# Two stacked transformer blocks on one core: weights in units of two K tiles, x loaded first, and a first layer in five phases

## The chip, the cores and the metric

One core of a Trainium2 chip runs the whole program. The metric is the device time of one execution in microseconds (us). TensorE (PE in the rows) multiplies, VectorE (DVE) and ScalarE (ACT) work on elements, GpSimd (POOL) does little here, and SyncE (SP) issues nearly all loads, in one queue and in order.

## The reference

The input `x` is 256 tokens by 2048 features in float32. Two layers of a first block and two layers of a second block follow each other. The change is in the first block, whose layers begin like this:

```python
mod = jax.nn.silu(c) @ w_mod + b_mod                  # 2048 -> 3 * 2048, one row for all tokens
shift, scale, gate = jnp.split(mod, 3, axis=-1)
h = rms_norm(x, g_pre) * (1.0 + scale[:, None, :]) + shift[:, None, :]
proj = h @ w_in                                       # 2048 -> 5648 columns
...                                                   # attention, gating and linear attention on parts of proj
out = y @ w_out
return x + gate[:, None, :] * rms_norm(out, g_post)
```

The second block has attention of three kinds and an MLP (`w_up`, `w_down`); its share of the time is the larger one, and its code is only re-indented by the change.

## The kernel before, in words

The 2048 features are 16 K tiles of 128. A product needs a K tile of `h` (feature-major, `hT`) and the same K tile of the weight. Weights come as float32 by loads of two K tiles by 512 columns (512 KB) into `raw`, a ring of five buffers. ScalarE rounds a load to `hi` (L265), VectorE takes `lo = raw - hi` (L266), and TensorE adds three products (L287 to L289: hi, lo, and hi with the low half of `hT`). A few K tiles of layer 0, `WHOLE0 = (3, 7, 11, 14, 15)`, are multiplied whole in float32 instead (L325), without a split.

`shift`, `scale` and `gate` are products of one row with `w_mod`, by a generator `gemv`. Each of its loads goes into `rawm`, a ring of two buffers, or, ahead of the first phase, into `raw`. VectorE multiplies each K tile of the load by a scalar of `sc` and adds it to `gacc` (L493, the first of a row by L491). When all 16 K tiles of the input are in, TensorE sums `gacc` over partitions (L498), and VectorE adds the bias (L507, `mod`). A variant, `gemv_pe`, lets TensorE do the whole product (L523).

Layer 0 of the first block runs its input product in phases of K tiles: `[(0,), (4,), (8,), (12,)]`, where 4 stands for K tiles 4 to 7. In each phase but the last, eleven column chunks of `w_in` (nine of 512 columns, two of 264) are multiplied. The first phase copies its sums out of PSUM on ScalarE (L819), each later one adds them on VectorE (L821, 24 instructions a phase: 18 of 512 columns and 6 narrower ones). Three chunks before the end of a phase, `enter(p + 1)` drains the background work, starts the `gemv` loads for the K tiles of the phase after, transposes `x` (L747), scales it (L751, `h`) and makes `hT` (L755, L759, L760), which needs `scale` for L751 and `shift` for the rest. `pump`, called after each unit of weights, gives out background loads at a set rate. The last phase has all chunks and the mixing between them.

Ahead of the first phase, `scale` for K tiles 0 to 3 is made by `gemv` on VectorE, `shift` for K tiles 0 and 1 by `gemv_pe`, `x` is loaded behind twelve of these loads, and `shift` for K tiles 2 and 3 follows by `gemv`. A list scheduler sets the order of instructions on each engine when the program is built, so the order isn't that of the code.

Of the kernel before, what the change touches and what calls it, by code (L numbers as in the profile page):

```python
# [21 lines left out]
P = 128  # L22
# [68 lines left out]
def kernel(  # L91
# [44 lines left out]
    # ---------------------------------------------------------------- constants  # L136
# [19 lines left out]
    # vectors that scale features, feature-major  # L156
# [3 lines left out]
    def fm_load(g, parts, on=None):  # L160
        """parts: (names, [rows, 128] AP); the rows become columns of fm, from 128 g on."""
# [31 lines left out]
    # vectors along the free axis  # L193
# [36 lines left out]
    # ---------------------------------------------------------------- helpers  # L230
# [13 lines left out]
    def put(dst, ps, scale=None):  # L244
        """dst (hi | lo) from a [128, 256] view of PSUM."""
# [23 lines left out]
    def w_unit(w, k0, n0, n, whole=()):  # L269
        """4 K tiles x n columns of w, split but for those in whole; yields (kt, [(hi [128, n], lo), ...])."""  # L270
        for k in range(k0, k0 + 4, 2):
            raw = raw_tile()
            nc.sync.dma_start(
                out=raw[:, :2 * n].rearrange("p (k n) -> p k n", k=2),
                in_=w[k * P:(k + 2) * P, n0:n0 + n].rearrange("(k p) n -> p k n", p=P))
            js = [j for j in range(2) if k + j not in whole]
            parts = [(raw[:, j * n:(j + 1) * n], None) for j in range(2)]
            if js:
                o = js[0] * n
                hi, lo = split(raw[:, o:o + len(js) * n], len(js) * n)  # L280
                for i, j in enumerate(js):
                    parts[j] = hi[:, i * n:(i + 1) * n], lo[:, i * n:(i + 1) * n]
            yield (k, parts)

    def three(ps, xa, xb, wh, wl, first, last):
        """(xa + xb)^T (wh + wl) onto ps."""
        PE.matmul(ps, lhsT=xa, rhs=wh, start=first, stop=False)  # L287
        PE.matmul(ps, lhsT=xa, rhs=wl, start=False, stop=False)  # L288
        PE.matmul(ps, lhsT=xb, rhs=wh, start=False, stop=last)  # L289

    late = []
    AGE = 3

    def settle(age=0):
        """the last step of each gemv whose loads were all given out at least age pumps ago."""
        while late and bg["n"] - late[0][0] >= age:
            late.pop(0)[1]()
# [19 lines left out]
    def gemm_chunk(w, xT, units, n0, n, after_unit=None, whole=()):  # L317
        ps = [bank(mm) for _ in range(2)]
        for k0 in units:
            for kk, pairs in w_unit(w, k0, n0, n, whole):  # L320
                for t in range(2):
                    for j, (wh, wl) in enumerate(pairs):
                        a = xT[kk + j]
                        if wl is None:
                            PE.matmul(ps[t][:, :n], lhsT=a[:, t * P:(t + 1) * P], rhs=wh, start=kk + j == units[0],  # L325
                                      stop=kk + j == units[-1] + 3)
                            continue
                        three(ps[t][:, :n], a[:, 0, t * P:(t + 1) * P], a[:, 1, t * P:(t + 1) * P],
                              wh, wl, kk + j == units[0], kk + j == units[-1] + 3)
# [31 lines left out]
    def turn(srcs, eng, m=None, tag="k"):  # L361
        """transposes of up to 4 [128, 128] APs, side by side."""
# [10 lines left out]
    def y_turn(dst, ytm):  # L373
        """ytm: per token tile a [128, 512]; dst: 4 act tiles."""
# [10 lines left out]
    def x_done(t, n):  # L385
        """the sum of squares of a finished 512-column piece of x."""
# [10 lines left out]
    # rotary tables of the first block  # L397
# [61 lines left out]
    def rotate(buf, nh, cos2, sin2, hf):  # L459
        """in place on buf [128, nh, 2 * hf]; sin2 = (-sin | sin)."""  # L460
# [52 lines left out]
    def gemv_pe(l, part, k0, nk, tag, pb):  # L513
        """the same on the tensor engine, a K tile of the result after the other, into a bank."""
        for i in range(nk):
            n0 = part * D + (k0 + i) * P
            for u in range(0, KT, 8):
                raw = raw_tile(tag)
                nc.sync.dma_start(
                    out=raw.rearrange("p (k n) -> p k n", k=8),  # L520
                    in_=w_mod[l, u * P:(u + 8) * P, n0:n0 + P].rearrange("(k p) n -> p k n", p=P))
                for k in range(8):
                    PE.matmul(pb[:, i:i + 1], lhsT=raw[:, k * P:(k + 1) * P], rhs=sc[:, u + k:u + k + 1],  # L523
                              start=(u + k == 0), stop=(u + k == KT - 1))
                yield

    # ---------------------------------------------------------------- first block
# [9 lines left out]
    def swa(l, cc, q, kv, kT, zs, yT):  # L537
        """heads 8 cc .. 8 cc + 7."""
# [832 lines left out]
```

## Time and profile before

| what | us |
|---|---|
| three timed runs | 3045.58, 3048.32 (median), 3050.96 |
| span of the profiled execution | 3045.1 |
| TensorE busy in that span | 2953.5 (97%) |
| VectorE busy | 1984.3 (65%) |
| ScalarE busy | 1436.1 (47%) |

The profiled execution is known by its span, from the first to the last instruction; its own time lies between that and the runs beside it, the median of which is 3.2 above the span. Shares of busy time are means over all stages. A busy TensorE isn't one at its peak, since the ends of its pipelined products are modelled.

### The profile page before, as it was taken

The page shows a single profiled execution, that of the slowest core. Times are in us where ns is not written, and L with a number is a line of the kernel's source. Part 1 is how long each engine was busy: PE and PEld are TensorE (multiplying, and loading weights), DVE is VectorE, ACT ScalarE, POOL GpSimd, SP SyncE. Part 2 cuts the span into 40 slices and gives each one's busy share as a digit, 9 for nine tenths or more (in the row PEclk, how much of TensorE's full clock was granted, in tenths as well). Part 3 has the DMA queues.
Part 4 walks back from the last instruction along what each step waited for, and adds up shares of the span by engine and source line. Part 5 has one row for each costly group of instructions (what it writes and reads, how often), then busy time and mean ns, then how long its engine had stood idle before and what let it go on. Part 6 is the DMA issues. An engine that isn't in the chain of part 4 may idle for free.

```text
span 3045.1 us, 40015 instructions
## 1 busy us (share of the span) xinstructions
PE 2953.5 (97%) x15042; PEld 2442.3 (80%) x15042; DVE 1984.3 (65%) x2832; ACT 1436.1 (47%) x2271; POOL 36.3 (1%) x56
## 2 busy tenths in 40 slices
PE   6999998999999999999999999999999999999998
PEld 5676676887787887888888888888788888888887
DVE  5888877788766555565666656656555665656655
ACT  2334545445556555454444444455554444444444
POOL 0000000000000000000000000000000000000000
PEclk9999998999999999999999999999999999999999
DMA  8898588898454655565665566554556666555564
GB/s 286 291 317 291 184 266 288 279 309 269 123 180 146 180 145 163 175 188 192 189 191 188 190 190 190 190 173 135 166 165 199 192 188 190 190 190 190 188 191 153
DMA packets 318072, 617.57 MB, mean 203 GB/s; under 512 B 20233, under 2 KB 48069, under 8 KB 317877
## 3 DMA queue, kind: packets, MB, share of 16 engines
q1 hardware_dynamic: 317220, 614.40, 63.4%
q8 instruction: 118, 1.93, 0.3%
q0 software_dynamic: 336, 0.49, 0.1%
q14 instruction: 78, 0.63, 0.1%
q10 hardware_dynamic: 320, 0.12, 0.0%
HBM read 610.73 MB, written 4.19 MB: 202 GB/s over the span
## 4 chain that ended last, share of the span: by engine, by line
PE 80%; DMA 8%; DVE 7%; issue 2%; ACT 2%; POOL 0%; SPq 0%; DVEq 0%; ACTq 0%; POOLq 0%
PE b L288 16%; PE b L289 16%; PE b L287 16%; PE b L1190 16%; PE b L1192 8%; DMA rawm<-in_w_mod_dram 5%; DVE gacc L493 2%; DVE lo L266 2%; PE b L325 1%; DMA raw<-in_w_in_dram 1%; PE b L366 1%; ACT hi L265 1%; PE b L564 1%; PE b L952 1%; PE b L551 0%
## 5 line engine op out<-in xcount | busy, mean ns | idle before, releaser
L266 DVE TENSOR_TENSOR lo<-raw,hi 128x1024 fp32r<-128x1024 f32 (+4 forms) x964 | 1126.6, 1170 | 799.0 <-ACT hi L265 795.7
L265 ACT CAST hi<-raw 128x1024 fp32r<-128x1024 f32 (+4 forms) x964 | 972.7, 1009 | 1313.5 <-PE b L289 758.1
L287 PE MATMUL b<-hi,act 128*128 128x512 f32 (+2 forms) x2728 | 1072.9, 394 | 9.2 <-DVE pr L821 2.6
L288 PE MATMUL b<-lo,act 128*128 128x512 f32 (+2 forms) x2728 | 1047.7, 384 | 6.9 <-DVE lo L266 6.8
L289 PE MATMUL b<-hi,act 128*128 128x512 f32 (+2 forms) x2728 | 1045.5, 384 | 0.3 <-DVE act L252 0.3
L1190 PE MATMUL b<-act,hi 128*128 128x512 f32 x2048 | 721.0, 397 | 0.0
L287 PEld LDWEIGHTS b<-hi,act 128*128 128x128 f32 x2728 | 515.1, 189 | 121.2 <-issue 16.4
L288 PEld LDWEIGHTS b<-lo,act 128*128 128x128 f32 x2728 | 515.7, 189 | 117.1 <-DVE lo L266 11.7
L289 PEld LDWEIGHTS b<-hi,act 128*128 128x128 f32 x2728 | 514.9, 189 | 98.1 <-issue 1.2
L1192 PE MATMUL b<-act,lo 128*128 128x256 f32 x2048 | 574.9, 281 | 0.0
L1190 PEld LDWEIGHTS b<-act,hi 128*128 128x128 f32 x2048 | 384.4, 188 | 92.8
L1192 PEld LDWEIGHTS b<-act,lo 128*128 128x128 f32 x2048 | 386.9, 189 | 0.5
L493 DVE SCALAR_TENSOR_TENSOR gacc<-rawm,sc,gacc 128x1024 f32<-128x1024 f32 (+1 forms) x210 | 220.9, 1052 | 57.7 <-DMA rawm<-in_w_mod_dram 56.2
L325 PE MATMUL b<-raw,act 128*128 128x512 f32 (+1 forms) x240 | 111.0, 561 | 0.0
L1208 DVE SCALAR_TENSOR_TENSOR act<-b,s,act 128x512 f32<-128x512 f32 x128 | 90.0, 744 | 5.7 <-PE b L289 5.7
L354 ACT ACTIVATE s<-s,s 128x128 f32<-128x128 f32 (+3 forms) x144 | 64.1, 447 | 40.3 <-DVE s L351 39.3
L241 POOL TENSOR_TENSOR s<-s,cs 128x1 f32<-128x1 f32 (+1 forms) x38 | 27.6, 730 | 2909.0 <-DVE s L239 2709.3
L325 PEld LDWEIGHTS b<-raw,act 128*128 128x128 f32 x240 | 43.8, 191 | 17.9 <-issue 11.8
L1200 DVE SCALAR_TENSOR_TENSOR h<-h 128x256 f32<-128x256 f32 x128 | 54.4, 425 | 4.4
L821 DVE TENSOR_TENSOR act<-b,act 128x512 f32<-128x512 f32 (+2 forms) x82 | 51.4, 632 | 8.2 <-PE b L325 7.4
L390 ACT ACTIVATE junk<-act 128x512 bf16<-128x512 f32 x56 | 35.1, 626 | 40.2 <-DMA act<-in_x_dram 21.1
L1198 DVE TENSOR_TENSOR h<-b,h 128x256 f32<-128x256 f32 x128 | 53.4, 417 | 0.0
(268 smaller groups left out, 1666.7 us busy)
## 6 DMA issues: line engine op xcount, KB each, us to landing
raw<-in_w_in_dram SPq DMA_DIRECT2D x256, 512.0 KB, 4.8
raw<-in_w_up_dram SPq DMA_DIRECT2D x256, 512.0 KB, 3.7
raw<-in_w_down_dram SPq DMA_DIRECT2D x256, 512.0 KB, 3.6
rawm<-in_w_mod_dram SPq DMA_DIRECT2D x176, 512.0 KB, 4.8
raw<-in_w_out_dram SPq DMA_DIRECT2D x64, 512.0 KB, 4.7
raw<-in_w_o_dram SPq DMA_DIRECT2D x64, 512.0 KB, 3.7
raw<-in_w_in_dram SPq DMA_DIRECT2D x32, 288.0 KB, 2.9
raw<-in_w_in_dram SPq DMA_DIRECT2D x32, 264.0 KB, 4.7
```

Source lines behind the costliest of these rows:

```text
L265: A.copy(out=hi[:, :n], in_=src)
L266: V.tensor_tensor(out=lo[:, :n], in0=src, in1=hi[:, :n].bitcast(F32), op=SUB)
L287: PE.matmul(ps, lhsT=xa, rhs=wh, start=first, stop=False)
L288: PE.matmul(ps, lhsT=xa, rhs=wl, start=False, stop=False)
L289: PE.matmul(ps, lhsT=xb, rhs=wh, start=False, stop=last)
L325: PE.matmul(ps[t][:, :n], lhsT=a[:, t * P:(t + 1) * P], rhs=wh, start=kk + j == units[0], stop=kk + j == units[-1] + 3)
L354: A.activation(out=s[:, h, :], in_=s[:, h, :], func=AF.Exp, bias=nm[:, h:h + 1], accum_out=den[:, h:h + 1])
L493: eng.scalar_tensor_tensor(out=acc, in0=w, scalar=sc[:, u + k:u + k + 1], in1=acc, op0=MUL, op1=ADD)
L1190: PE.matmul(ps[f], lhsT=wh[:, f * P:(f + 1) * P], rhs=a.rearrange("p a b -> p (a b)"), start=(kk + j == 0), stop=False)
L1192: PE.matmul(ps[f][:, S:], lhsT=wl[:, f * P:(f + 1) * P], rhs=a[:, 0, :], start=False, stop=(kk + j == KT - 1))
L1200: V.scalar_tensor_tensor(out=s2, in0=s, scalar=0.0, in1=s, op0=MAX, op1=MUL)
L1208: V.scalar_tensor_tensor(out=xc, in0=ps, scalar=r2[t], in1=xc, op0=MUL, op1=ADD)
```

## The change

Five things change.

- `w_unit`, four K tiles in two loads, becomes `w_pair`, two K tiles in one load. Loads, splits and products are the same; `pump` is now called after every two K tiles, and the rates (`UN1`, `RATE0`, `RATE1`) and `AGE` are set so that a K tile gives out as much as before.
- Layer 0 runs in five phases: K tiles 0 and 1; 2 and 3; 4 to 7; 8 to 11; 12 to 15.
- `x` is loaded ahead of all `w_mod`.
- Ahead of the first phase, `scale` and `shift` are made for K tiles 0 and 1 alone, `scale` by `gemv` on VectorE, `shift` by a new `gemv_pe` with two columns groups a load. Together they take 8 loads in place of 16.
- `scale` and `shift` of K tiles 2 and 3 become the background of the first phase (8 loads, each of four K tiles by 256 columns), those of K tiles 4 to 7 the background of the second (16 loads), and so on.

```diff
@@ the rate of background work, and its age
-    AGE = 3
+    AGE = 6
@@ gemm_chunk
-        for k0 in units:
-            for kk, pairs in w_unit(w, k0, n0, n, whole):
-                for t in range(2):
...
+        for kk in units:
+            pairs = w_pair(w, kk, n0, n, whole)
+            for t in range(2):
...
@@ shift on the tensor engine
-    def gemv_pe(l, part, k0, nk, tag, pb):
-        for i in range(nk):
-            n0 = part * D + (k0 + i) * P
-            for u in range(0, KT, 8):
...
+    def gemv_pe(l, part, k0, tag, pbs):
+        nk = len(pbs)
+        n, n0 = nk * P, part * D + k0 * P
+        per = 1024 // n
...
+        for u in range(0, KT, per):
+            raw = raw_tile(tag)
...
+            for k in range(per):
+                for i in range(nk):
+                    PE.matmul(pbs[i][:, 0:1], lhsT=raw[:, k * n + i * P:k * n + (i + 1) * P],
+                              rhs=sc[:, u + k:u + k + 1], start=(u + k == 0), stop=(u + k == KT - 1))
+            yield
@@ prepare0
-        if p == 0:
-            background(mods(0, 1, (4, 4)) + mods(0, 0, (4, 4)), 16 / UN0)
...
+        if p < 4:
+            if p == 1:
+                fill_rope()
+                fill_vectors()
+            k0, nk = ((2, 2), (4, 4), (8, 4), (12, 4))[p]
+            pumps = 8 * len(PHASES0[p])
+            background(mods(0, 1, (k0, nk)) + mods(0, 0, (k0, nk)), 4 * nk / (1.125 * pumps))
@@ the start
-    UN0 = 9
-    UN1 = 24
-    RATE1 = 48
-    NPE = 2
-    RATE0 = 31
+    PHASES0 = [(0,), (2,), (4, 6), (8, 10), (12, 14)]
+    UN1 = 48
+    RATE1 = 96
+    RATE0 = 62
...
-    pb = bank()
-    scale, shift = mods(0, 1, (0, 4), tag="raw")[0], gemv_pe(0, 0, 0, NPE, "raw", pb)
+    x_load(x[0])
+    pbs = [bank() for _ in range(2)]
+    scale, shift = mods(0, 1, (0, 2), tag="raw")[0], gemv_pe(0, 0, 0, "raw", pbs)
     for i in range(4):
         next(scale)
         next(shift, None)
+    for n in range(4):
+        for t in range(2):
+            x_done(t, n)
     fill_fm(None)
     run([scale])
-    x_load(x[0])
-    for n in range(4):
-        for t in range(2):
-            x_done(t, n)
-    run([gemv(0, 0, NPE, 4 - NPE, V, "raw", pb[:, NPE:])])
-    mod_done(0, 0, 0, 4, pb)
+    for i in range(2):
+        mod_done(0, 0, i, 1, pbs[i])
...
-        block1(0, [(0,), (4,), (8,), (12,)], SPLIT0, ORDER, prepare0, lambda: None, WHOLE0)
+        block1(0, PHASES0, SPLIT0, ORDER, prepare0, lambda: None, WHOLE0)
```

What the scheduler makes of it is seen in the order of instructions. First the load queue (SyncE) at the start of the program, before; `raw` tiles of L485 are `scale` by `gemv`, those of L519 `shift` by `gemv_pe`, `act` tiles are pieces of `x`:

```order
L168 DMA y_88<-in_c_dram 16x128
L485 DMA raw_104<-in_w_mod_dram 128x2x512
L519 DMA raw_108<-in_w_mod_dram 128x8x128
...
L485 DMA raw_187<-in_w_mod_dram 128x2x512
L154 DMA act_198<-in_x_dram 128x512
...
L485 DMA raw_244<-in_w_mod_dram 128x4x256
L273 DMA raw_307<-in_w_in_dram 128x2x512
```

The same place now (L484 is `gemv`, L521 `gemv_pe`, L272 `w_in`):

```order
L168 DMA y_88<-in_c_dram 16x128
L154 DMA act_101<-in_x_dram 128x512
...
L154 DMA act_115<-in_x_dram 128x512
L484 DMA raw_121<-in_w_mod_dram 128x4x256
L521 DMA raw_128<-in_w_mod_dram 128x4x256
...
L521 DMA raw_176<-in_w_mod_dram 128x4x256
L272 DMA raw_258<-in_w_in_dram 128x2x512
```

All eight pieces of `x` now stand ahead of eight loads of `w_mod`, where twelve stood ahead of `x` and four behind it.

Second, TensorE at the start, before: L523 is `shift`, L173 transposes vectors, L747 `x`, L768 spreads the reciprocal norms, L425 transposes the positions, L208 the rows of `sg_b`, one instruction a layer:

```order
L523 MATMUL b_101<-sc,raw_108 128x1 x8
L173 MATMUL b_163<-cs,y_160 128x128
L173 MATMUL b_172<-cs,y_166 128x104
L523 MATMUL b_101<-sc,raw_122 128x1 x8
L523 MATMUL b_101<-sc,raw_136 128x1 x8
L523 MATMUL b_101<-sc,raw_150 128x1 x8
L747 MATMUL b_276<-cs,act_198 128x128
...
L425 MATMUL b_694<-cs,y_692 128x2
L208 MATMUL b_738<-cs,y_736 128x8
L208 MATMUL b_743<-cs,y_741 128x8
```

And now (L526 is `shift`, L771 and L424 what L768 and L425 were):

```order
L526 MATMUL b_118<-sc,raw_128 128x1
L173 MATMUL b_199<-cs,y_196 128x128
L173 MATMUL b_208<-cs,y_202 128x104
L771 MATMUL b_232<-h_233,cs 128x128
L771 MATMUL b_232<-h_236,cs 128x128
L424 MATMUL b_513<-cs,y_511 128x2
L208 MATMUL b_557<-cs,y_555 128x8
L208 MATMUL b_562<-cs,y_560 128x8
L526 MATMUL b_117<-sc,raw_144 128x1
```

The spreading of the norms, the positions and both `sg_b` transposes moved from behind all four loads of `shift` to a place between the first and the second of them.

Third, VectorE where the first half of a phase of four K tiles comes ready: `mod_0` is `shift`, `act` with L760 the low half of `hT` of K tiles 4 to 6. Before, the 19th of the 22 `w_in` loads of the phase ahead is split (`lo_823`) just before it:

```order
L493 SCALAR_TENSOR_TENSOR gacc_562<-rawm_680,sc,gacc_562 128x512
L455 COPY rope<-s_725 128x8 x2
L751 SCALAR_TENSOR_TENSOR h_771<-b_761,mod_1_102,rb_274 128x256
L266 TENSOR_TENSOR lo_823<-raw_820,hi_822 128x1024
L507 TENSOR_TENSOR mod_0_224<-b_684,fm 128x4
L491 TENSOR_SCALAR gacc_809<-rawm_810,sc 128x512
L266 TENSOR_TENSOR lo_841<-raw_838,hi_840 128x512
L760 SCALAR_TENSOR_TENSOR act_753<-h_751,mod_0_224,act_753 128x256
```

Now (L492 is the accumulation, L824 the addition, L506 the bias, L763 the low half of `hT`), for the same K tiles:

```order
L266 TENSOR_TENSOR lo_951<-raw_948,hi_950 128x512
L492 SCALAR_TENSOR_TENSOR gacc_736<-rawm_789,sc,gacc_736 128x512
L824 TENSOR_TENSOR act_636<-b_923,act_636 128x512
L266 TENSOR_TENSOR lo_973<-raw_970,hi_972 128x1024
...
L824 TENSOR_TENSOR act_670<-b_947,act_670 128x512
L492 SCALAR_TENSOR_TENSOR gacc_736<-rawm_815,sc,gacc_736 128x512
L266 TENSOR_TENSOR lo_995<-raw_992,hi_994 128x512
L266 TENSOR_TENSOR lo_1017<-raw_1014,hi_1016 128x1024
L492 SCALAR_TENSOR_TENSOR gacc_736<-rawm_839,sc,gacc_736 128x512 x2
L506 TENSOR_TENSOR mod_0_127<-b_870,fm 128x4
L763 SCALAR_TENSOR_TENSOR act_883<-h_881,mod_0_127,act_883 128x256
```

`lo_951` belongs to the last `w_in` load of the second phase, `lo_973`, `lo_995` and `lo_1017` already to the third, which needs this `shift`: it now comes behind all splits and all 24 additions of the phase ahead.

From the first `h` (L751, now L754) to this `shift`, VectorE's queue held, before, 30 accumulations of 512 columns and 13 of 256 with 2 that begin a row, 19 splits and no addition. It now holds 30 of 512 and 30 of 256 with 4 that begin a row, 25 splits (11 of 1024 columns, 2 of 528, 10 of 512, 2 of 264), 24 additions, 11 instructions of 256 columns on `h` and `hT`, and some 35 small ones.

## Rows read from the trace of the kernel before

**Rows 1.** The page, busy time of each engine, share of the span, instructions.
```profile
PE 2953.5 (97%) x15042; PEld 2442.3 (80%) x15042; DVE 1984.3 (65%) x2832; ACT 1436.1 (47%) x2271; POOL 36.3 (1%) x56
```

**Rows 2.** Windows: stretch, length, busy per engine, clock, DMA share, GB/s.
```profile
0.00:50.50 50.50, 24.16 (x106) 21.94 (x106) 26.15 (x59) 11.39 (x25) 4.17 (x11) 1.00 0.91 284
50.50:117.30 66.80, 65.02 (x271) 47.29 (x270) 51.50 (x102) 30.46 (x55) 0.00 (x0) 1.00 0.88 298
117.30:184.40 67.10, 63.47 (x259) 45.63 (x258) 55.80 (x88) 19.25 (x28) 0.00 (x0) 0.97 0.86 291
184.40:245.80 61.40, 61.30 (x264) 45.21 (x263) 55.25 (x85) 17.67 (x26) 0.00 (x0) 1.00 0.92 316
```

**Rows 3.** Timeline: start, length, what; first product, last additions of two phases.
```profile
50.47 0.78 PE L287 MATMUL b<-hi,act 128*128 128x512 f32 x1
...
184.41 0.68 DVE L821 TENSOR_TENSOR act<-b,act 128x512 f32<-128x512 f32 x1
...
245.75 0.69 DVE L821 TENSOR_TENSOR act<-b,act 128x512 f32<-128x512 f32 x1 [0.87 <-PE b L325]
```

**Rows 4.** TensorE's waits, 50 to 246: total, times, longest; first and last of six.
```profile
PE b L287 <- DVE act L821: 1.8, 2, 1.6
...
PE b L747 <- DVE mod L507: 0.3, 1, 0.3
```

**Rows 5.** Waits of VectorE and of the load queue, 50 to 246; landing of `rawm`.
```profile
DVE lo L266 <- ACT hi L265: 12.2, 15, 2.0
DVE gacc L493 <- DMA rawm<-in_w_mod_dram: 10.9, 12, 2.4
DVE act L821 <- PE b L325: 5.4, 8, 1.9
...
SPq L485 <- DVE gacc L493: 86.0, 45, 4.8
...
DMA to landing us min/median/max: 3.7/4.4/7.5
```

**Rows 6.** Timeline of the start; the last row is the landing of `sg_b`.
```profile
9.90 3.54 PE L523 MATMUL b<-sc,raw 128*128 128x1 f32 x16 [5.56 <-DMA raw<-in_w_mod_dram]
13.31 0.63 PE L173 MATMUL b<-cs,y 128*128 128x128 f32 x2
14.05 0.51 POOL L206 DMA_DIRECT2D y<-in_sg_b_dram  x1 [4.79 <-PE b L173]
38.29 0.48 DVE L751 SCALAR_TENSOR_TENSOR h<-b,mod,rb 128x256 f32<-128x256 f32 x1
49.70 0.16 DVE L507 TENSOR_TENSOR mod<-b,fm 128x4 f32<-128x4 f32 x1 [1.10 <-PE b L498]
...
DMA to landing us min/median/max: 4.4/4.7/5.0
```

**Rows 7.** Groups on VectorE, 184.4 to 245.8; the last row 0 to 50.5.
```profile
L493 DVE SCALAR_TENSOR_TENSOR gacc<-rawm,sc,gacc 128x512 f32<-128x512 f32 x23 | 17.1, 745 | 1.8 <-DMA rawm<-in_w_mod_dram 1.6
L821 DVE TENSOR_TENSOR act<-b,act 128x512 f32<-128x512 f32 x17 | 11.7, 687 | 2.4 <-PE b L325 2.3
L266 DVE TENSOR_TENSOR lo<-raw,hi 128x1024 fp32r<-128x1024 f32 x9 | 11.0, 1218 | 0.2 <-ACT hi L265 0.2
...
L266 DVE TENSOR_TENSOR lo<-raw,hi 128x512 fp32r<-128x512 f32 x8 | 5.5, 685 | 0.7 <-ACT hi L265 0.5
...
L493 DVE SCALAR_TENSOR_TENSOR gacc<-raw,sc,gacc 128x256 f32<-128x256 f32 x15 | 7.2, 480 | 0.1
```

**Rows 8.** TensorE after a wait: one timeline row, then a window as in rows 2.
```profile
149.10 0.39 PE L287 MATMUL b<-hi,act 128*128 128x264 f32 x1 [1.58 <-DVE act L821]
...
147.00:153.00 6.00, 4.42 (x22) 3.91 (x20) 4.90 (x10) 1.51 (x2) 0.00 (x0) 0.72 0.79 264
```

**Rows 9.** TensorE's waits from 246 to 1000, the largest of 21.
```profile
PE b L288 <- DVE lo L266: 6.1, 6, 1.9
```

**Rows 10.** A window as in rows 2, in layer 1.
```profile
900.00:950.00 50.00, 50.00 (x244) 41.83 (x244) 25.13 (x33) 27.02 (x42) 0.00 (x0) 1.00 0.65 204
```

More of the change, by code (lines that the diff above doesn't have):

```diff
@@ L267, in split, with w_pair @@
         return hi, lo
[L269 to L283, printed above, removed]
+    def w_pair(w, k, n0, n, whole=()):
+        raw = raw_tile()
+        nc.sync.dma_start(
+            out=raw[:, :2 * n].rearrange("p (k n) -> p k n", k=2),
+            in_=w[k * P:(k + 2) * P, n0:n0 + n].rearrange("(k p) n -> p k n", p=P))
+        js = [j for j in range(2) if k + j not in whole]
+        parts = [(raw[:, j * n:(j + 1) * n], None) for j in range(2)]
+        if js:
+            o = js[0] * n
+            hi, lo = split(raw[:, o:o + len(js) * n], len(js) * n)
+            for i, j in enumerate(js):
+                parts[j] = hi[:, i * n:(i + 1) * n], lo[:, i * n:(i + 1) * n]
+        return parts
     def three(ps, xa, xb, wh, wl, first, last):
@@ L318, in gemm_chunk @@
         ps = [bank(mm) for _ in range(2)]
-        for k0 in units:
-            for kk, pairs in w_unit(w, k0, n0, n, whole):
-                for t in range(2):
[L322 to L329, printed above, removed]
+        for kk in units:
+            pairs = w_pair(w, kk, n0, n, whole)
+            for t in range(2):
+                for j, (wh, wl) in enumerate(pairs):
+                    a = xT[kk + j]
+                    if wl is None:
+                        PE.matmul(ps[t][:, :n], lhsT=a[:, t * P:(t + 1) * P], rhs=wh, start=kk + j == units[0],
+                                  stop=kk + j == units[-1] + 1)
+                        continue
+                    three(ps[t][:, :n], a[:, 0, t * P:(t + 1) * P], a[:, 1, t * P:(t + 1) * P],
+                          wh, wl, kk + j == units[0], kk + j == units[-1] + 1)
             if after_unit:
@@ L511, in mod_done @@
             V.tensor_tensor(out=o, in0=o, in1=fv(("gpost", l), k0, nk), op=MUL)
-    def gemv_pe(l, part, k0, nk, tag, pb):
-        for i in range(nk):
-            n0 = part * D + (k0 + i) * P
-            for u in range(0, KT, 8):
[L518 to L525, printed above, removed]
+    def gemv_pe(l, part, k0, tag, pbs):
+        nk = len(pbs)
+        n, n0 = nk * P, part * D + k0 * P
+        per = 1024 // n
+        if (l, part) not in mod:
+            mod[l, part] = const.tile([P, KT], F32, name=f"mod{l}_{part}")
+        for u in range(0, KT, per):
+            raw = raw_tile(tag)
+            nc.sync.dma_start(
+                out=raw.rearrange("p (k n) -> p k n", k=per),
+                in_=w_mod[l, u * P:(u + per) * P, n0:n0 + n].rearrange("(k p) n -> p k n", p=P))
+            for k in range(per):
[3 more added lines that the diff above has]
+            yield
     def swa_keys(kv):
@@ L853, in enter @@
             prepare(p)
-            for k0 in phases[p]:
-                make_hT(l, k0 // 4, rb, hT, whole)
+            for k in phases[p]:
+                make_hT(l, k, rb, hT, whole)
         enter(0)
@@ L960, in block2 @@
     def block2(l, xT, r):
-        units = (0, 4, 8, 12)
+        units = tuple(range(0, KT, 2))
         mix = {}
```

72 lines of the change are left out of this document (33 added, 39 removed).

## The prediction, made before the run

> **What bounds the kernel now.** The page comes first: TensorE is busy for 2953.5 of 3045.1 us [rows 1], so 91.6 us are open in the whole program. The windows by stage come second. Before the first product of layer 0, at 50.5, TensorE is idle for 26.3 us, more than a quarter of all that is open; in the three phases that follow it is busy for 65.0 of 66.8, 63.5 of 67.1 and 61.3 of 61.4 us [rows 2]. I set the ends of the phases at their last copies or additions, 117.3, 184.4 and 245.8 [rows 3]. The reader should see two more things in those windows: the DMA share is 0.86 to 0.92, and VectorE is busy for 51.5, 55.8 and 55.3 us, so three resources run close to each other.
>
> The waits come third. From 50 to 246 TensorE waits for 5.6 us in all, over six kinds of wait [rows 4]; it sets the pace, by a narrow margin. VectorE waits for hi casts, for `rawm` loads and for TensorE, some 31 us together. The load queue issued 53 `rawm` loads there, and 45 times it stood until VectorE was done with a buffer, 86 us in all; a load then takes 4.4 us to land [rows 5]. So both `rawm` buffers are always in use, and the modulation can't run ahead by itself: it goes as fast as VectorE empties them.
>
> A head start of TensorE is therefore worth something only if VectorE's modulation for the next phase is ready earlier too. That is what I work out.
>
> **The start.** Removed: eight `w_mod` loads, 4.2 MB, ahead of the first phase. Moved: `x`. Before, `h` begins at 38.29, but `shift` for K tiles 2 and 3 is only there at 49.70, and the first product follows [rows 3, 6].
>
> Now, step by step. The constants and `x`, 2.3 MB, at the 284 GB/s of the first stretch [rows 2] take 8.1 us from the first issue, at about 1.7: all landed at 9.8. Two `w_mod` loads more, 1.05 MB, 3.7 us: 13.5. The first load of `shift` keeps TensorE for 3.5 us, as one did before (16 records) [rows 6]: 17.0. Then TensorE's order has the two L173, and six small instructions, the second L208 among them, ahead of the other loads of `shift`. That L208 needs the second `sg_b` load, which GpSimd gave out 0.74 us after L173 began and which takes at least 4.4 us to land [rows 6]: 17.0 + 0.7 + 4.7 = 22.4. Behind this wait stand twenty-four matmuls of three `shift` loads, and behind them the load queue, as the fourth load takes the buffer that the second one frees. The second load's products end at 25.9; the fourth load is given out then and lands 4.4 to 4.7 later, at about 30.6; the third load's products and a few transposes fill the time to 30.3; the fourth's end at 34.1. Half a microsecond for L497 and about 0.9 for five short VectorE instructions brings `h` to 35.5. One `h`, one activation and one hi cast later, at about 37.5, comes the first product. The head start of TensorE is 50.5 - 37.5 = 13.0 us. Bounds: 33 for `h` if `sg_b` isn't waited for, 38.5 if loads land in the longest 7.5 us of [rows 5]. Note that `h` itself is only 2.8 us earlier than before: for VectorE there is hardly a head start.
>
> **Phases one and two.** TensorE's work doesn't change: two phases of two K tiles are what one of four was, about 61 us. VectorE's does. Up to the `shift` that the third phase (K tiles 4 to 7) waits for, the order counts, at the group times per instruction of [rows 7]: 30 accumulations of 512 columns at 0.745 and 2 beginnings at 0.48, 23.3 us; 30 of 256 columns at 0.48 and 2 at 0.35, 15.1; 11 splits of 1024 columns at 1.22, 10 of 512 at 0.685, and 4 narrow ones at 0.70 or 0.43, 22.5; 24 additions, 18 at 0.687 and 6 narrower, 14.3; 11 on `h` and `hT` at 0.48, 5.3; 35 small ones at 0.17, 5.9. The sum is 86.4 us of group time. The 24 additions are the new phase's; that the modulation of K tiles 2 and 3 is done in 256 columns adds another 3.5.
>
> How fast is group time worked off? From 184.4 to 245.8 all seventeen groups add up to 61.6 us, in 61.4 us, 55.3 of them busy [rows 2, 7] (neighbours overlap a little). So the pace was 1.0 there, with VectorE 90% busy; without any gap it would be 61.6 / 55.3 = 1.115, and at the 83% of the phase before, 0.93. The new stretch resembles the 90% one: TensorE can't hold VectorE back, but `rawm` can, because in the second phase 16 loads belong to chunks that take TensorE half as long as before. I take 1.0. The third phase is then ready at 35.5 + 86.4 + 0.5 for one activation = 122.4, against a start at 117.3 before: 5.1 us later. Bounds: 35.5 + 77.5 + 0.5 = 113.5 (3.8 earlier) and 35.5 + 92.9 + 0.5 = 128.9 (11.6 later).
>
> The order shows the same from the other side: the `shift` that came before the last three splits of the old phase now comes behind all of them. TensorE will be through with the second phase and wait.
>
> **The clock.** After a wait of 1.58 us at 149.10 the granted clock was 0.72 over 147 to 153, that is 1.2 GHz for over half of it [rows 8]; at half speed for 3.4 us, 1.7 us are lost. I put 1.5 us for the wait ahead of the third phase (0 to 3).
>
> **The rest.** From the third phase on the work is what it was from the second phase of before, 128.5 us of TensorE's pace to the last phase [rows 3]: 0, with 3 either way, since TensorE's waits there are a few us in all. The finer units give out loads twice as often at half the rate; the same `lo` splits, copies and loads hide behind TensorE's products. All that smoother feeding could save from 246 to 1000 is the waits for `lo`, 6.1 us [rows 9]; half of it at best, so 0, and 3 for the range.
>
> **Sum.** 5.1 + 1.5 = 6.6 us on the profiled 3045.1, 3051.7. The runs' median stands 3.2 above that span: 3048.3 + 6.6 = 3055 us. A measurement of this kernel tells 0.2%, 6.1 us, from no change; the forecast is slower, just outside it.
>
> **A rule against the first reading.** Busy TensorE alone would say that it is the bound in the phases. Its weight loads were busy for 47.3 of 66.8, 45.6 of 67.1 and 45.2 of 61.4 us, 0.68 to 0.74, and for 0.84 where it runs in layer 1 with VectorE half idle [rows 2, 10]. The Trainium skill (Perfetto Trace Analysis, Identifying the Most-Contended Engine) says that matmul busy time is a bad measure and that the busy share of weight loads shows TensorE's headroom. By that TensorE has some 15% left in the phases, VectorE is the bound throughout, and the third rival below is the forecast. The waits of [rows 4] say otherwise, and whole K tiles (L325) keep TensorE longer for each weight load.
>
> **Rivals.**
>
> No change. VectorE runs the new stretch at a pace between 1.0 and 1.115, because its waits for TensorE are gone: at 1.06, 35.5 + 81.5 + 0.5 = 117.5, level with before, and 1 for the clock: 3049 us. For it: 5.4 us of VectorE's waits were for TensorE [rows 5]. Against it: `rawm` waits grow.
>
> Faster. It takes both a start without the `sg_b` wait (33) and VectorE without gaps: 33 + 77.5 + 0.5 = 111, 6.3 earlier, and the later phases 4 us shorter as VectorE enters them ahead: 3048.3 - 10.3 = 3038 us. It decides from a pace above 1.1. TensorE alone would give the whole 13 us; VectorE can't follow that, by its own sum. For it: the prologue's waits are my longest guess.
>
> Slower by more. VectorE sets the pace through all phases, not only the first two. From the first `h` to the last addition of the phase of K tiles 8 to 11 the orders count 191.8 us of group time before, passed in 208.1 us (38.29 to 245.75 and its 0.69) [rows 3, 6], and 216.5 now; at that pace 234.9 us, from 35.5 to 270.4, 24 later: 3072 us. Against it: TensorE, not VectorE, made that pace.
>
> **How the numbers follow.** Slower as summed 0.35, slower by more 0.08, no change 0.36, faster 0.21. The likeliest direction is slower, 0.43, and its time 3055. Its own range is 3052 to 3063. The range that leaves out 2 in 10 at most goes from 3038, the faster rival's middle, to 3066, short of the last rival: 3038 to 3066.
>
> **What would show it.** First product at 36 to 39. TensorE standing at the second L208 until about 22. VectorE over 88% busy from 40 to 122, with no wait for TensorE. TensorE waiting for `shift` several us just before the third phase, and a clock of 1.2 GHz after that. First product of the third phase at 120 to 126, and 128 us from there to the last phase. The prediction is wrong if the third phase begins before 115, or if the later phases are shorter than before by more than 4 us.

## The result and the profile after

| | before | after |
|---|---|---|
| median of the runs beside each other, us | 3049.64 (3045.58 to 3051.85, 4 runs) | 3079.6 (3070.46 to 3091.11, 4 runs) |
| ratio, 95% interval | | 1.0106, 1.0076 to 1.0136 |
| a second set, other runs, us | 3052.54 (29 runs) | 3075.72 (3071.3 to 3086.93, 6 runs) |
| ratio, 95% interval | | 1.0088, 1.0061 to 1.0114 |
| span of the profiled execution, us | 3045.1 | 3089.4; in the second set 3075.3 |

The change makes the kernel slower, by 0.9 to 1.1%; the medians are 30.0 us apart in the first set and 23.2 in the second. The direction was forecast, the size was not: 6.6 us were forecast, and the time lies outside the range. The profiled execution of after is its slowest run; where the second profile (span 3075.3) differs, the text says so.

The page of after: busy times, and of the forty slices the granted clock and the DMA share.

```profile
PE 2977.3 (96%) x15042; PEld 2460.7 (80%) x15042; DVE 1999.5 (65%) x2876; ACT 1435.0 (46%) x2271; POOL 41.1 (1%) x56
...
PEclk9899999899999999999999999999999999999999
DMA  7798668888555555466666666554556666655554
```

TensorE has the same 15042 instructions as in [rows 1]. It is busy for 23.8 us more, as some of its time ran at a lower clock, and the first two slices have a DMA share of 7 (tenths), where the page of before has 8.

The windows by stage, as [rows 2]. The ends are the first product (41.89), the last copy of the first phase (84.40), the first product of K tiles 4 to 7 (134.72), and the last additions of the two phases from there on. The last two rows are the stretch around 134 and everything up to the first addition of K tiles 4 to 7.

```profile
0.00:41.89 41.89, 21.30 (x95) 19.43 (x95) 11.52 (x39) 9.36 (x23) 4.42 (x11) 1.00 0.70 216
41.89:84.40 42.51, 35.97 (x146) 28.32 (x147) 35.11 (x86) 22.20 (x41) 0.00 (x0) 0.92 0.81 272
84.40:134.72 50.32, 39.09 (x130) 24.05 (x128) 40.61 (x71) 8.87 (x15) 0.00 (x0) 0.89 0.83 278
134.72:202.20 67.48, 65.71 (x266) 47.96 (x267) 59.58 (x98) 19.87 (x29) 0.00 (x0) 0.96 0.83 278
202.20:268.00 65.80, 62.11 (x265) 45.23 (x264) 57.29 (x87) 17.06 (x24) 0.00 (x0) 1.00 0.89 298
125.00:140.00 15.00, 8.28 (x24) 6.17 (x23) 8.81 (x15) 2.75 (x5) 0.00 (x0) 0.68 0.78 268
...
0.00:142.20 142.20, 103.84 (x387) 77.42 (x388) 91.58 (x202) 42.20 (x80) 4.42 (x11) 0.92 0.76 248
```

The reader should see three things. The two half phases take 92.8 us (41.89 to 134.72) for the products that took 66.8 before. In them TensorE is idle for 17.8 us and runs at clocks of 0.92 and 0.89, where the phase of before had 1.00 and 1.8 us idle [rows 2]. And the loads moved 216 GB/s before the first product, not 284.

TensorE's waits in the two half phases, the largest three (in before, all waits from 50 to 246 were 5.6 us):

```profile
PE b L497 <- DVE gacc L492: 5.9, 1, 5.9
PE b L497 <- DVE s L416: 4.1, 1, 4.1
PE b L286 <- DVE act L824: 2.8, 4, 0.9
```

L497 sums the accumulators of the modulation. The wait of 4.1 us, at 71.2, is for the `shift` of K tiles 2 and 3, that of 5.9 us, at 126.1, for the `shift` of K tiles 4 to 7. In both the DMA engines were busy throughout:

```profile
71.00:75.00 4.00, 0.18 (x1) 0.00 (x0) 3.78 (x10) 0.62 (x1) 0.00 (x0) 1.00 1.04 369
126.10:132.00 5.90, 0.04 (x1) 0.00 (x0) 4.58 (x6) 0.26 (x1) 0.00 (x0) 0.87 1.01 363
```

The timeline of TensorE at the second one:

```profile
125.11 1.02 PE L324 MATMUL b<-raw,act 128*128 128x512 f32 x2
132.06 1.87 PE L497 MATMUL b<-cs,gacc 128*128 128x1 f32 x8 [5.93 <-DVE gacc L492]
134.72 0.79 PE L286 MATMUL b<-hi,act 128*128 128x512 f32 x1 [0.79 <-ACT act L762]
135.32 0.63 PE L287 MATMUL b<-lo,act 128*128 128x512 f32 x1
```

A product of 512 columns takes 0.63 us there and some 0.39 us from 142 on: after the wait TensorE ran at 1.2 GHz.

Where the 44.3 us between the two profiled spans arise, and the 30.2 of the second profile, is a sum over 110 windows of 10 us: time in which TensorE was not busy, and what the granted clock took (10 us times one minus the clock, of each window).

| stretch, us | idle before / after / second | clock before / after / second |
|---|---|---|
| 0 to 140 | 29.8 / 38.4 / 39.7 | 0.0 / 11.6 / 12.0 |
| 140 to 270 | 4.8 / 5.4 / 3.9 | 2.2 / 0.3 / 1.7 |
| 270 to 1100 | 37.1 / 48.8 / 45.7 | 21.6 / 35.8 / 22.1 |

The first row is nearly the same in both profiles of after, 20 and 22 us more than before. The third isn't: 26 us more in one, 9 in the other.

### The profile page after: what moved, and what is told of

Its sections match the earlier page's. It is cut to its first block, busy times and chain, and to the rows that moved or that the text cites. A ratio compares the mean times of both kernels' runs of the same rounds, so it can differ in the third digit from the quotient of the medians.

```text
span 3089.4 us, 40052 instructions
## 1 busy us (share of the span) xinstructions
PE 2977.3 (96%) x15042; PEld 2460.7 (80%) x15042; DVE 1999.5 (65%) x2876; ACT 1435.0 (46%) x2271; POOL 41.1 (1%) x56
## 4 chain that ended last, share of the span: by engine, by line
PE 81%; DMA 8%; DVE 6%; ACT 2%; issue 2%; POOL 0%; SPq 0%; ACTq 0%; DVEq 0%; POOLq 0%
PE b L287 16%; PE b L288 16%; PE b L286 16%; PE b L1193 15%; PE b L1195 8%; DMA rawm<-in_w_mod_dram 6%; DVE gacc L492 2%; PE b L324 1%; DVE lo L266 1%; DMA raw<-in_w_in_dram 1%; PE b L365 1%; ACT hi L265 1%; PE b L567 1%; PE b L497 1%; PE b L955 1%
## 5 line engine op out<-in xcount | busy, mean ns | idle before, releaser
L266 DVE TENSOR_TENSOR lo<-raw,hi 128x1024 fp32r<-128x1024 f32 (+5 forms) x964 | 1126.3, 1170 | 802.7 <-ACT hi L265 800.1
L265 ACT CAST hi<-raw 128x1024 fp32r<-128x1024 f32 (+5 forms) x964 | 972.5, 1009 | 1328.7 <-PE b L288 753.9
L287 PE MATMUL b<-lo,act 128*128 128x512 f32 (+2 forms) x2728 | 1058.8, 388 | 9.1 <-DVE lo L266 8.9
L492 DVE SCALAR_TENSOR_TENSOR gacc<-rawm,sc,gacc 128x1024 f32<-128x1024 f32 (+2 forms) x240 | 235.0, 979 | 61.0 <-DMA rawm<-in_w_mod_dram 59.2
L324 PE MATMUL b<-raw,act 128*128 128x512 f32 (+1 forms) x240 | 113.1, 570 | 0.0
L824 DVE TENSOR_TENSOR act<-b,act 128x512 f32<-128x512 f32 (+2 forms) x102 | 63.7, 631 | 4.7 <-PE b L324 3.7
L257 DVE TENSOR_TENSOR act<-h,act 128x256 fp32r<-128x256 f32 x128 | 50.8, 418 | 0.0
```

Of the source, the lines that this page charges most:

```text
L265: A.copy(out=hi[:, :n], in_=src)
L266: V.tensor_tensor(out=lo[:, :n], in0=src, in1=hi[:, :n].bitcast(F32), op=SUB)
L492: eng.scalar_tensor_tensor(out=acc, in0=w, scalar=sc[:, u + k:u + k + 1], in1=acc, op0=MUL, op1=ADD)
L824: V.tensor_tensor(out=o, in0=a, in1=o, op=ADD)
```

## The experiments

Ratios are to runs of the kernel before on the same chip; not all rows are from the same chip. "First addition" is that of the phase after the first four K tiles: 121.3 in before, 142.2 and 141.2 in the two profiles of after.

| kernel | median us | ratio, 95% interval | first product | first addition | MB by then |
|---|---|---|---|---|---|
| before, the profiled execution | | | 50.5 | 121.3 | 35.5 |
| finer units alone | 3051.48 | 0.9997, 0.9982 to 1.0013 | 50.5 | 123.0 | 35.3 |
| `x` first alone | 3058.12 | 1.0018, 1.0001 to 1.0036 | 57.7 | 128.0 | 35.6 |
| five phases, 16 loads ahead | 3062.23 | 1.0039, 1.0025 to 1.0052 | 58.2 | 130.7 | 35.4 |
| after, again | 3075.72 | 1.0088, 1.0061 to 1.0114 | 42.1 | 141.2 | 35.3 |
| after, small work later | 3073.35 | 1.0059, 1.0037 to 1.0081 | 38.4 | 134.1 | 35.3 |
| after, `x` behind | 3068.68 | 1.0050, 1.0035 to 1.0064 | 34.8 | 131.6 | 35.8 |
| after, both of these | 3069.52 | 1.0062, 1.0042 to 1.0082 | 36.3 | 135.0 | 35.8 |
| after, fewer accumulations | 3071.62 | 1.0058, 1.0039 to 1.0078 | 41.7 | 137.0 | 35.5 |
| after, fewer loads | 3061.36 | 1.0030, 1.0014 to 1.0046 | 41.5 | 127.5 | 29.1 |
| after, fewer of both | 3048.53 | 0.9993, 0.9976 to 1.0010 | 42.5 | 113.1 | 29.2 |
| after, three `rawm` | 3057.57 | 1.0016, 1.0004 to 1.0028 | 41.0 | 131.5 | 35.2 |
| after, `x` behind, three `rawm` | 3045.46 | 0.9983, 0.9971 to 0.9996 | 35.1 | 126.5 | 35.3 |
| finer units, three `rawm` | 3041.46 | 0.9969, 0.9957 to 0.9981 | 50.9 | 120.1 | 36.6 |
| before, three `rawm` | 3033.45 | 0.9941, 0.9925 to 0.9958 | 52.0 | 120.8 | 36.7 |

The MB are the GB/s of the window from 0 to the first addition times its length: for after 248 by 142.2 is 35.3 MB.

**Which part of the change costs what.** Finer units alone:

```diff
-    PHASES0 = [(0,), (2,), (4, 6), (8, 10), (12, 14)]
+    PHASES0 = [(0, 2), (4, 6), (8, 10), (12, 14)]
...
-    x_load(x[0])
...  the start and prepare0 of before, at half its rates
```

> Only the finer units: four phases of four K tiles and the old start, but weights in units of two K tiles, the pump after every two, the rates halved. Theory 1 (the loss is made in the two half phases, where VectorE's modulation and 24 more additions don't fit, and the later losses follow from a later and slower-clocked start): within 6 us of before, first product at 50, first additions at 121 as before. Theory 2 (the finer units themselves cost something from 330 us on, where the trace after loses another 24 us): slower by 10 to 25 us, with the loss between 330 and 960, and waits of TensorE for the modulation of layer 1 there.

No difference: theory 2 falls. Only `x` moved, in the kernel before:

```diff
+    x_load(x[0])
     pb = bank()
     scale, shift = mods(0, 1, (0, 4), tag="raw")[0], gemv_pe(0, 0, 0, NPE, "raw", pb)
...
     run([scale])
-    x_load(x[0])
```

> Only x loaded ahead of all w_mod, in the kernel before; 16 w_mod loads still precede the first phase. Theory 1: the loads ahead of the first product are the same bytes, so the first product stays within 4 us of 50.5 and the time within 6 us of before. Rival: the second sg_b row holds TensorE up among the loads of shift as in the trace after, first product 3 to 6 us later and the time the same 3 to 6 us longer.

Slower by some 5.5 us, just outside no change; the first product is 7.2 us later, more than either expectation. Five phases with all sixteen loads ahead of the first:

```diff
-    x_load(x[0])
-    pbs = [bank() for _ in range(2)]
-    scale, shift = mods(0, 1, (0, 2), tag="raw")[0], gemv_pe(0, 0, 0, "raw", pbs)
+    x_load(x[0])
+    pb = bank()
+    scale, shift = mods(0, 1, (0, 4), tag="raw")[0], gemv_pe(0, 0, 0, 2, "raw", pb)
...
-            k0, nk = ((2, 2), (4, 4), (8, 4), (12, 4))[p]
+            k0, nk = ((4, 4), None, (8, 4), (12, 4))[p]
```

> Five phases and finer units, x first, but scale and shift of K tiles 0 to 3 all made before the first phase (16 loads), so that the background of the first two phases is that of K tiles 4 to 7 alone. What remains of the change in the two half phases is 24 more additions on VectorE, 16.5 us of group time. Theory 1: no wait of TensorE between the two half phases, a wait of at most 3 us ahead of K tiles 4 to 7, and 3050 to 3060 us. Rival (the half phases cost for themselves, by additions and by half the products for each copy out of PSUM): 3065 us or more, with TensorE waiting for VectorE throughout both.

The time lies between theory and rival. In the half phases the theory holds: from 58.2 to 131 TensorE waits for 2.2 us in all, none of it for the modulation, and the first addition is only 2.7 us later than with `x` first alone. By the ratios five phases with 24 more additions cost some 6 us (1.0039 less 1.0018), but the two intervals overlap, so this part is not clear of 0. And the kernel after once more:

> The kernel after, unchanged, for a second profile and more runs. Its four runs spread over 21 us. Theory 1: the loss ahead of K tiles 4 to 7 (first addition of that phase at 142, 21 later than before) is there again within 2 us, as it comes from the order of work. What is not there again of the later losses (24 us from 330 to 960) belongs to single waits and the granted clock after them, not to the change's first phases. Rival: the loss of the first phases changes from run to run as well, by 5 us or more.

The first phases repeat within 1 us, 141.2 and 142.2. The steps so far: finer units 0, `x` first 5 to 6 us, five phases 6, and the narrow start, eight loads of the modulation moved from ahead of the first phase into it, some 15 (1.0088 less 1.0039). Only the last is large against the intervals; at the first addition it is 11.5 us (142.2 less 130.7).

**The start.** The load queue of after, its `w_mod` loads into `raw` from 12 to 36 us (start, length; the third word is the queue):

```profile
12.49 3.11 SPq L484 DMA_DIRECT2D raw<-in_w_mod_dram  x1
22.22 0.37 SPq L521 DMA_DIRECT2D raw<-in_w_mod_dram  x1
22.70 0.44 SPq L484 DMA_DIRECT2D raw<-in_w_mod_dram  x1
31.05 0.37 SPq L521 DMA_DIRECT2D raw<-in_w_mod_dram  x1
```

The five `raw` buffers are given out by 12.5. The sixth load is given out at 22.22, when TensorE is through with the first load of `shift`, the eighth at 31.05, when it is through with the second. What was given out has landed by then, so the loads stop at 22 and from 27.3 to 31.5, as the DMA share of after from 0 to 42 us in forty slices shows:

```profile
DMA  0198795288968999999930699200002995598999
```

Before, and in the next kernel, the eight pieces of `x` are what the queue has to load while `raw` is full. After with `x` behind:

```diff
-    x_load(x[0])
     pbs = [bank() for _ in range(2)]
...
     run([scale])
+    x_load(x[0])
```

> The kernel after, with x loaded behind the eight w_mod loads of the start instead of ahead of them, as its only change. If x first costs 7.6 us of the first h, as in the kernel before with only x moved, then here the first h comes at 31 to 34 in place of 39.9, the first product at 33 to 36, K tiles 4 to 7 begin 6 to 8 us earlier, and the time is 3066 to 3070 us. Rival: x itself is what h waits for, as only eight loads stand ahead of it; then h stays within 2 us and nothing changes.

As expected in every number but one, K tiles 4 to 7, which come 10.6 us earlier. The same forty slices of this kernel, DMA share from 0 to 42 us, have no idle stretch of that length:

```profile
DMA  0298998999992189858999899999999999877830
```

The small work moved out of the half phases:

```diff
-            if p == 1:
+            if p == 3:
                 fill_rope()
                 fill_vectors()
```

> The kernel after, with fill_rope and fill_vectors in the background step before the last phase instead of before the second one. About 30 small VectorE instructions (5 us of group time) leave the two half phases, and both L208 leave the start. Theory 1 (VectorE's order of work sets the start of K tiles 4 to 7): first product 2 to 4 us earlier than 41.9 as TensorE doesn't stand at the second L208, and the first product of K tiles 4 to 7 at about 126 in place of 134.7; 3068 us. Rival A (the w_mod loads through two rawm buffers set it): only the 2 to 4 us of the start. Rival B: the work is only moved to a place that is as tight, 0 us in the end.

The first product came 3.5 us earlier, the first addition 8.1, and the time at 3073 is closer to after than expected. Both edits together:

> The kernel after with x behind the eight w_mod loads and fill_rope and fill_vectors moved to the step before the last phase: both gains of the two runs together, if they add up (7 and 2 to 7 us): first product at 33, first addition of K tiles 4 to 7 at 125 to 130, 3060 to 3066 us. If they pay for the same wait: as x moved alone, 3068.

They don't add up; the first addition is even 3.4 us later than with `x` behind alone.

**VectorE's work or the loads.** Work left out: each load for K tiles 2 to 7 is accumulated for its first K tile only.

```diff
-            for k in range(per):
+            for k in range(1 if l == 0 and part < 2 and k0 in (2, 4) else per):
                 w = raw[:, k * n:(k + 1) * n]
```

> Work left out: of each w_mod load for K tiles 2 to 7 of layer 0 only the first K tile is accumulated, which takes 40 accumulations, 23 us of group time, off VectorE ahead of K tiles 4 to 7; all loads stay. Theory 1 (VectorE's work): TensorE's waits between the half phases and ahead of K tiles 4 to 7 all but vanish, that phase begins at 108 to 115, 3050 us or less. Rival A (the loads): it begins at 125 or later, 3065 us or more.

This is where my theory fell. `shift` for K tiles 4 to 7 is there at 115.7 in place of 134.0, as theory 1 said; yet the first addition comes at 137.0, 5 us earlier. Now TensorE waits for the `hi` casts of `w_in`, from 41.89 to 134.8:

```profile
PE b L286 <- ACT hi L265: 11.4, 10, 2.8
PE b L287 <- DVE lo L266: 2.8, 4, 1.3
```

And the load queue, from 41.89 to 134.72, waits longest for loads into the `rawm` buffers to land (10.5 us in after), and less than in after for VectorE (35.9 us there):

```profile
SPq L484 <- DMA rawm<-in_w_mod_dram: 27.4, 19, 3.4
SPq L484 <- DVE gacc L492: 21.4, 17, 4.2
```

The queue is in order, so `w_in` loads stand behind a `w_mod` load that waits for its buffer. Next, half of these loads left out, all accumulations kept:

```diff
+            if l > 0 or part == 2 or k0 not in (2, 4) or u // per % 2 == 0:
                 raw = raw_tile(tag)
                 nc.sync.dma_start(
```

> Work changed: in the modulation of K tiles 2 to 7 of layer 0 every second load is left out and its accumulations read the load before it once more; VectorE's work stays, 12 loads (6.3 MB) fewer stand ahead of K tiles 4 to 7. New theory L (the loads set the time from the start to K tiles 4 to 7: in all kernels so far 35.4 to 35.7 MB had been moved when that phase's first addition came, at 121 to 142 us): the first addition comes 10 to 20 us earlier than 142, and the time falls to 3060 or less. Theory 1 (VectorE's work): within 3 us of 142, 3070 or more.

The first addition moves by 14.7 us, three times as far, though the time of 3061 is just above the 3060 that theory L named. Both left out:

> Work left out on both sides: half of the loads and 40 of the accumulations for K tiles 2 to 7 of layer 0. If loads and VectorE's work together hold TensorE up, it is now left alone: two half phases of 61 us from 42, first addition of K tiles 4 to 7 at 107 to 112, and 3045 us or less. If a third thing holds it (hi casts on ScalarE, the ring of raw, the clock), 120 or later.

First addition at 113.1, 29 us earlier than after, more than the two apart. Nothing else holds TensorE up for long; from 41.89 to 134.72 it is now busy all but 2.2 us, at full clock:

```profile
41.89:134.72 92.83, 90.61 (x378) 66.12 (x379) 77.95 (x153) 38.55 (x67) 0.00 (x0) 1.00 0.84 282
```

The time, 3048.5, is that of before and not the 3045 or less expected: 8 us of lead at the first addition are gone by the end. In its profile, which is of its longest run (span 3056.0), it has 5 us more idle time than before from 270 to 1100 us, and 14 more of clock.

**A third buffer.**

```diff
-    BUFS = {"act": 40, "pr": 6, "s": 4, "pT": 3, "y": 4, "k": 6}
+    BUFS = {"act": 39, "pr": 6, "s": 4, "pT": 3, "y": 4, "k": 6}
...
-        return wp.tile([P, 1024], F32, tag=tag, bufs={"raw": 5, "rawm": 2}[tag], name=f"{tag}{next(uid)}")
+        return wp.tile([P, 1024], F32, tag=tag, bufs={"raw": 5, "rawm": 3}[tag], name=f"{tag}{next(uid)}")
```

> The kernel after with three rawm buffers and 39 act buffers. Theory L, with the load queue standing in front of a full rawm: the rate of loads from 40 to 60 us rises from 240 to 280 GB/s or more, and K tiles 4 to 7 begin 4 to 8 us earlier. Theory 1 (VectorE's work): its 6 us of waits for rawm fall, 1 to 5 us earlier. If the queue's waits at rawm only follow VectorE's pace: 0.

The first addition is 10.7 us earlier and the time 18 us shorter, with all work done: more than theory L expected, though the rate from 40 to 60 us rose to 270 GB/s only, not 280. (The room can't come from `pr`: with five of these for six the kernel deadlocks.) TensorE's waits from 41.89 to 134.8 for the modulation are gone; it waits for `w_in` (first the `hi` cast, then `lo`):

```profile
PE b L286 <- ACT hi L265: 7.7, 6, 2.6
PE b L287 <- DVE lo L266: 4.8, 6, 1.3
```

The load queue still stands at L484 for 58 us of this stretch (64 in after), but for loads to land only 2.7 us in place of 10.5.

Is that particular to the changed order?

> The kernel before with three rawm buffers and 39 act buffers. If the two rawm buffers cost the kernel after 18 us because only there the loads decide, the kernel before gains little, 0 to 5 us, as TensorE was busy for 61 to 65 us of each phase. If they cost every phase alike, 10 us or more are gained here as well, to 3040 or less.

It is not. The kernel before gains as much, 0.59%, and this version beats both kernels. The windows of its three first phases, as the last three of [rows 2], the second and third to its own last additions:

```profile
50.50:117.30 66.80, 65.90 (x275) 48.39 (x275) 55.13 (x107) 31.40 (x55) 0.00 (x0) 1.00 0.92 316
117.30:179.80 62.50, 61.57 (x264) 45.33 (x263) 55.67 (x89) 19.91 (x27) 0.00 (x0) 1.00 0.91 311
179.80:241.80 62.00, 62.00 (x268) 46.14 (x267) 56.33 (x83) 17.78 (x25) 0.00 (x0) 1.00 0.95 326
```

The second phase takes 62.5 us in place of 67.1, and the loads move 316, 311 and 326 GB/s in place of 298, 291 and 316. In this first block TensorE waits less, and the second block begins 17 us earlier (945.8 in place of 962.9). The Trainium skill (Perfetto Trace Analysis, Optimization Strategy) says that the same gap repeating on the engine that should be saturated can mean that there is not enough room for the next tile, by the number of buffers for one. The trace agrees in part: the gap stood on the load queue, not on an engine. Its 45 waits for VectorE, 86.0 us, in [rows 5] are now fewer, from 50 to 246 as there:

```profile
SPq L485 <- DVE gacc L493: 59.9, 33, 5.7
```

The changed kernels with three buffers:

> The kernel after with x behind the eight w_mod loads and with three rawm buffers. If the two pay for different waits (7 us of the start, 18 us of the loads), 3046 to 3053 us, level with before, and the first addition of K tiles 4 to 7 at 122 to 127. If the start is of no use as long as the loads decide (the same 35.5 MB must come first), 3055 to 3060 as with three buffers alone.

The two add up to 3045.5, level with before or a little better, just under the 3046 expected. But against before with three buffers it is still 12 us slower, although its first product comes 17 us earlier: the first additions are at 126.5 and 120.8. And the finer units:

> The finer units alone (four phases, the old start) with three rawm buffers. If finer pumps need a third buffer to be worth anything, 3040 us or less; if four phases are bound by TensorE, within 5 us of before.

Neither: 3041.5, faster than before, but 8 us slower than before with three buffers and units of four K tiles.

So the third buffer speeds both kernels up and leaves their difference nearly as it was: with three buffers after is still 24 us slower than before (3057.57 and 3033.45; 1.0016 less 0.9941). By the ratios `x` in front has some 10 us of that, the finer units 9, the five phases and the narrow start the last 4. With two buffers the finer units cost nothing and the narrow start the most: what an edit costs depends on the ring behind it.

## Why the prediction was right in direction and wrong in size

**The start** was mis-sized. `h` was forecast at 35.5 and came at 39.87, the first product at 37.5 and 41.89: a head start of 8.6 us, not 13.0, outside the 36 to 39 named as a sign. The wait at the second L208 is there, until 27.27 instead of 22.4, and so is the fourth load behind it, given out at 31.05 instead of 25.9. They are late by what stands ahead of them: the first load of `shift` had its products at 18.65 instead of 13.5.

```profile
1.71 7.76 SPq L154 DMA_DIRECT2D act<-in_x_dram  x8
9.99 0.51 SPq L521 DMA_DIRECT2D raw<-in_w_mod_dram  x1
...
18.65 3.54 PE L526 MATMUL b<-sc,raw 128*128 128x1 f32 x16 [10.00 <-DMA raw<-in_w_mod_dram]
...
27.27 0.24 PE L208 MATMUL b<-cs,y 8*128 8x8 f32 x1 [2.31 <-DMA y<-in_sg_b_dram]
27.44 3.57 PE L526 MATMUL b<-sc,raw 128*128 128x1 f32 x16
...
31.76 6.83 PE L526 MATMUL b<-sc,raw 128*128 128x1 f32 x32
...
1.70:13.50 11.80, 1.63 (x5) 0.86 (x5) 0.68 (x6) 5.72 (x14) 1.93 (x4) 1.00 0.77 207
1.70:18.65 16.95, 1.64 (x6) 0.90 (x6) 2.58 (x14) 7.46 (x19) 2.58 (x6) 1.00 0.86 253
```

The step that failed: I had let the loads move at 284 GB/s one after the other, 8.1 us for the constants and `x` and 3.7 for two loads of `w_mod`. In that time they moved at 207 GB/s. And they didn't come one after the other: `x` alone kept the queue until 9.47, five `w_mod` loads were given out from 9.51 on, and by 18.65 some 4.3 MB had been moved where the forecast counts 3.35. The idle stretch from 27.3 to 31.5 is not what made `h` late, as the forecast has that wait too. It holds back the loads of the first phase, and takes the rate of the start to 216 GB/s. The 284 of before were made with `x` filling the time in which `raw` is full; moved to the front it no longer does. The step asked what waits for `x`, not what `x` covers.

**Phases one and two.** The count of VectorE's work holds: the thirty groups of its rows from `h` to `shift` add up to 85.7 us, against 86.4 forecast. The step that failed is the pace: "I take 1.0". The window of after for that stretch:

```profile
39.87:134.00 94.13, 76.44 (x281) 53.35 (x279) 76.96 (x159) 32.02 (x55) 0.00 (x0) 0.91 0.83 277
```

85.7 in 94.1 us is a pace of 0.91, below the lower bound of 0.93, with VectorE 82% busy and not over 88. So K tiles 4 to 7 begin at 134.7, not 122.4: 4.4 us by the later `h`, 7.9 by the rest, nearly all of it pace. The rivals "no change" and "faster", which needed 1.06 and 1.1, fall with it. The bound was taken from phases in which 16 loads of the modulation pass through two buffers; in the half phases it is 24. In after, from 41.89 to 134.8, the load queue stood in front of them for 64 us of 93 (the seven kinds of wait at L484); the three longest of these:

```profile
SPq L484 <- DVE gacc L492: 35.9, 17, 4.3
SPq L484 <- DMA rawm<-in_w_mod_dram: 10.5, 8, 3.7
...
SPq L484 <- DVE s L411: 6.1, 2, 4.0
```

The prediction had seen that three resources run close, and that both `rawm` buffers are always in use, and then costed one resource only. The experiments show that neither VectorE's work nor the loads alone set the time: leaving out 40 accumulations is worth 5 us at the first addition, half of the loads 15, both 29, and a third buffer with all the work 11. In all kernels with the full work and two buffers 35.3 to 35.8 MB had been loaded when the first addition came. That alone proves little, since with the same work and one queue in order much the same has to be loaded by then, whatever holds it up; what shows the part of the loads is that the first addition moves when loads are left out or a buffer is added. Before moved them at 293 GB/s, 0.89 of the DMA engines' time, from the first microsecond; after at 248. TensorE's 26 idle us at the start, which the change sets out to use, were full of loads, and the phase behind them needed these loads. That eight of them come later doesn't make them fewer. How much of the pace is due to the shared ring, and how much to VectorE's order, the runs don't separate.

**The clock** was mis-sized as well: 1.5 us for one wait, measured 11.6 and 12.0 up to 140 us, as the waits were several, at 71 and 126 the longest. In the kernel with fewer of both, which has no such wait, it is 0.0.

**The later phases** were right. From the first addition of K tiles 4 to 7 to that of the last phase after takes 130.6 us (142.2 to 272.8), before 130.7 (121.3 to 252.0). That doesn't speak against the rival "slower by more", whose added work lies in the first two phases as well. Its number came close: 270.4 for the end of K tiles 8 to 11, which came at 268.7, and 3072 us, closer to the result than the forecast. Against its mechanism, VectorE as the one that sets the pace, speaks the kernel with fewer accumulations: 23 us of VectorE's work were taken away and 5 us came back. The rule of the Trainium skill (Perfetto Trace Analysis, Identifying the Most-Contended Engine) that leads to this rival is not borne out by that run.

**The finer pump** was right at 0 with two buffers.

**The rest of the program** was put at 0; whether it is stays open. From 270 to 1100 us the second profile has 8.6 us more idle time and 0.5 of clock, the first 11.7 and 14.2. But only one profile of before stands against them, and it is of a quick run. A profiled run of after takes 1.7 us more than its span; by that the span of 3045.1 is a run of 3046.8, 3 to 6 us below the two medians of before. Windows of after in which the clock fell:

```profile
430.00:450.00 20.00, 18.34 (x81) 15.80 (x80) 11.71 (x17) 5.38 (x8) 0.00 (x0) 0.74 0.44 147
520.00:570.00 50.00, 33.56 (x128) 26.62 (x128) 37.53 (x61) 24.56 (x48) 3.61 (x4) 0.73 0.73 234
...
1000.00:1020.00 20.00, 13.38 (x61) 11.87 (x62) 14.01 (x34) 13.03 (x33) 2.65 (x4) 0.66 0.15 43
```

The last two stand at the ends of layers, which before has too: at 500 to 550, clock 0.83, and at 950 to 980, clock 0.83. Whether an edit lengthens them was not settled: the other changed kernels with two `rawm` buffers show 4 to 19 us more than this profile of before in that stretch, in idle time and clock together, the finer units alone 4.

## What to carry to other kernels

Before idle time of one engine is counted as a gain, look at what the loads do in it: multiply the rate by the time up to the first work that needs them, and if the same bytes must come first in both orders, an earlier start of the engine may pay nothing, as here. A load that seems misplaced may be what the queue has to do while a ring of buffers is full. When an in-order load queue stands again and again in front of a ring of two, try a third buffer before moving work: here it was worth 17 us, and no reordering came near it.

## What was not expected of the hardware

The granted clock also fell to 1.2 GHz where TensorE had hardly waited. In the kernel after with three `rawm` buffers no wait between 300 and 440 us is longer than 1.1 us, and in the one with fewer loads and accumulations the longest step from one product to the next from 706 to 760 us is 1.05 us; yet the clock was half for all of one window of the first:

```profile
410.00:420.00 10.00, 10.00 (x42) 8.95 (x42) 5.75 (x13) 2.45 (x6) 0.00 (x0) 0.50 0.42 151
```

and for two thirds of one of the second:

```profile
720.00:740.00 20.00, 19.93 (x104) 16.75 (x103) 10.82 (x25) 7.43 (x22) 0.00 (x0) 0.66 0.51 158
```

TensorE is busy throughout, and half of its speed is gone for 10 us or more, which costs 5 us and over each time. What it did before, from 396 to 405 and from 709 to 723, was in large part short products, of 1 to 256 columns; that they are the cause is not shown. The loss is of the size of the differences measured here: the two profiles of after differ by 14.1 us, of which 11.9 are clock.
